# Four PSUM banks as one tile in rotation, and a gate spread in groups of eight tokens

## The chip, the cores and the metric

The kernel runs on one core of a Trainium2 chip. The metric is the device time of one execution in microseconds (us); smaller is better. The core has a matmul engine (TensorE, PE), which writes its results into PSUM, and VectorE (DVE), ScalarE (ACT) and GpSimd (POOL), which read them there. SyncE (SP) issues the transfers. PSUM has eight banks of 512 floats per partition. Each engine runs its own instructions in order and waits on semaphores for the others.

## The reference

A two-layer encoder over 256 tokens of width 1024. Layer 0 is differential attention and an expert mixer, layer 1 stick-breaking attention and an expert mixer. After each of the four parts comes a LayerNorm of `alpha * x + f(x)`. The expert mixer is the large part:

```python
q = (xt @ w_pq).reshape(T, PEER_HEADS, 2, PEER_HALF)
scores = jnp.einsum('thcd,hckd->thck', q, sub_keys).astype(jnp.float32)
s_top, i_top = lax.top_k(scores, PEER_TOPK)
cand = s_top[:, :, 0, :, None] + s_top[:, :, 1, None, :]
g_s, g_i = lax.top_k(cand.reshape(T, PEER_HEADS, PEER_TOPK * PEER_TOPK), PEER_TOPK)
expert_ids = jnp.take_along_axis(cand_ids.reshape(...), g_i, axis=-1)
gates = jax.nn.softmax(g_s, axis=-1)
...
h = jax.nn.gelu(jnp.einsum('td,ted->te', xblk, u_sel), approximate=False)
return jnp.einsum('te,ted->td', gb * h, v_sel)
```

Each token chooses 8 heads x 16 of 16384 experts (128 x 128 keys).

## The kernel before

The kernel computes the hidden values of all experts for all tokens, spreads the gates over a full 128 x 128 grid per token, and multiplies. A float32 product is done in three matmul passes: every weight tile is split into a high part `h` (ACT, L144) and a low part `l` (DVE or POOL, L149), and `h`, `l` and the low part of the input are multiplied in turn (L200 for products with 512 outputs, L245 for the query projection, L827, L840 and L842 for the hidden values). A matmul with `l` waits for the split.

PSUM is used through one pool with four buffers to a tag. Tag "w" serves the hidden values, the scores of the attention and the transposes of the LayerNorm; tag "acc" serves the accumulators of the projections and of the gather, the transposes of Q (L405), the V projection of layer 0 (L445, copied out by ACT in L449), two of the four head outputs of the attention (L505 and L507, read in L517 and L524), the routing scores (L674, copied by ACT in L675) and the gate spread. Each "acc" tile is one bank, and a new tile waits for the readers of the tile four before it. Most of the order of instructions is chosen by a scheduler; a few places are written out by hand.

Stages of a layer: attention, LayerNorm, query projection, then hidden values on PE with the routing on DVE beside them (scores, top 16 with MAX8, products, softmax), then the gate spread with more hidden values between, then the gather (L200 with weights `wh` and `wl`). A LayerNorm (L272 adds the accumulator, L275 and L294 are the statistics, L300 and L304 scale block 0 on ACT, L323 block 1 on DVE, L313 transposes) works on two blocks of 128 tokens. The matmuls before it are ordered so that block 0 is complete while the last matmuls of block 1 still run.

In the attention of layer 0, K is projected into "w" tiles while the rotary work on Q runs (L394 to L396 on DVE, L397 on POOL). Q is then transposed in four tiles, each of which is read by ACT (L407, the high part) and then DVE (L408, the low part). After K's projection comes V's (L445), and K's rotary work and transposes beside it.

The gate spread takes eight tokens at a time. DVE builds `oa` (L930: one where the key's second index matches), and `gh` and `gl` (L926: products of two small tables). PE multiplies them per token (L940, L941) into two accumulators of four tokens. The results of the last group are drained between `gh` and `gl` of the next: DVE multiplies the stored hidden values in (L899), ACT copies the rest (L900). The small tables (L913 to L916) are built for 16 tokens.

Of the kernel before, what the change touches and what calls it, by code (L numbers as in the profile page):

```python
# [20 lines left out]
P = 128  # L21
D = 1024
T = 256
# [35 lines left out]
def trunk(ctx: ExitStack, tc: tile.TileContext, x, xT, ln_g, ln_b, w_qkv, w_o_a, lam_p, subln, w_kv,  # L59
# [8 lines left out]

    big = bigp.tile([P, NE * T], F32, name="big")

    def reg(off, *shape):
# [16 lines left out]
    nc.vector.tensor_scalar(identb, jp, 0.0, None, OP.is_equal)  # L88
    ntri = const.tile([P, P], F32, name="ntri")
    nc.vector.tensor_scalar(ntri, jp, 0.0, -1.0, OP.is_le, OP.mult)  # L90
    none1 = const.tile([P, 1], F32, name="none1")
# [101 lines left out]
    def accs(tag):  # L193
        a = [[psum.tile([P, 512], F32, name=tag, tag=tag) for _ in range(NB)] for _ in range(2)]
        return [[a[f][b] for f in range(2)] for b in range(NB)]
# [38 lines left out]
    def stationary(xh, xl, src, tag, first=False):  # L234
        acc = [psum.tile([P, 2, T], F32, name=tag, tag=tag) for _ in range(4)]
        pre = units.prefetched() if first else []
        for d in range(DC):
            hl = pre[d] if d < len(pre) else units.get(src(d), "v" if first else "a", 1, units.after(d) if first else None)
            seq = [(n, q) for n in range(8) for q in range(2)] + [(n, 2) for n in range(8)]
            if first and d == 0:  # L240
                seq = [(n, q) for q in (0, 2, 1) for n in range(8)]
            for n, q in seq:
                w, a = hl[q // 2], (xh, xl, xh)[q]
                w, c = (w[n // 4], n % 4 * P) if isinstance(w, list) else (w, n * P)
                nc.tensor.matmul(acc[n // 2][:, n % 2, :], w[:, c:c + P], a[:, d, :],  # L245
                                 start=(d == 0 and q == 0 and n % 2 == 0),
                                 stop=(d == DC - 1 and q == 2), skip_group_check=True)
        return acc
# [127 lines left out]
    def diff_attention(xh, xl):  # L376
# [22 lines left out]
        def tr(srcv, dstT, tag):  # L399
            for i in range(4):  # L400
                pt = psum.tile([P, 2, T], F32, name=tag, tag=tag)
                for j in range(2):
# [96 lines left out]
        def s3(i):  # L499
            a = aT[i % 2]  # L500
            hs = slice(2 * i, 2 * i + 2)
            ps = psum.tile([P, 2, NB, P], F32, name="om", tag="acc" if i < 2 else "w")
            for j in range(2):
# [66 lines left out]

    def stick_breaking(xh, xl, yv, gb):
        QT, KT, V = reg(0, DC, T), reg(2048, DC, T), reg(4096, NB, D)
        spb = [reg(6144 + i * 512, 512) for i in range(4)]
# [75 lines left out]
    def peer(layer, xh, xl, spill, o_res):  # L649
# [16 lines left out]
        def scores(b):  # L666
            sc = reg(19456 + b * 2048, 2 * HP, NE)
            for g in range(4):
                ps = psum.tile([P, 4, NE], F32, name="acc", tag="acc")
                c = g % 2  # L670
                r = slice(c * 64, c * 64 + 64)
                for j in range(4):
                    h = 4 * (g // 2) + j
                    nc.tensor.matmul(ps[:, j, :], qp[r, h, b * P:(b + 1) * P], subk[r, h, :], start=True, stop=True)  # L674
                nc.scalar.activation(sc[:, 8 * (g // 2) + c:8 * (g // 2) + c + 7:2, :], ps, AF.Copy)  # L675
            return sc

        def routing(b, sc):
# [116 lines left out]
            yield 0.8  # L795
            pt = psum.tile([P, 4, P], F32, name="acc", tag="acc")
            for c in range(3):
# [85 lines left out]
        def extra():  # L883
            for i in range(N_STORED, N_STORED + N_EXTRA, 2):
                hx[i] = work.tile([P, 2 * T], F32, name="hx", tag="hw", bufs=RING)
                yield from hidden.pair(i, hx[i])

        ex = extra()
        nst = N_EXTRA * 24 - 48
# [5 lines left out]
        def drain():  # L895
            for t, ps in prev:
                pv = ps.rearrange("p t i -> p i t")
                wv = big.rearrange("p (i t) -> p i t", t=T)[:, :, t:t + 4]
                nc.vector.scalar_tensor_tensor(wv[:, 0:N_STORED], pv[:, 0:N_STORED], 1.0 / GS, wv[:, 0:N_STORED], OP.mult, OP.mult)  # L899
                nc.scalar.activation(wv[:, N_STORED:], pv[:, N_STORED:], AF.Copy, scale=1.0 / GS)  # L900

        i2 = iota2.unsqueeze(1).to_broadcast([P, 4, P, 2])
        NR = 8
        hi1, hi2, hi3 = (work.tile([P, NR, 8, 2], F16, name=n, bufs=1) for n in ("hi1", "hi2", "hi3"))
        lo = work.tile([P, NR, 16, 2], F16, name="lo", bufs=1)

        def parts(t0):
# [3 lines left out]

            i2 = iota2.unsqueeze(1).to_broadcast([P, NR, P, 2])
            nc.vector.tensor_tensor(hi1, i2[:, :, 0:8], col(1, 8), OP.is_equal)  # L913
            nc.vector.tensor_tensor(lo, i2[:, :, 0:16], col(2, 16), OP.is_equal)
            nc.vector.tensor_tensor(hi2, hi1, col(3, 8), OP.mult)
            nc.vector.tensor_tensor(hi3, hi1, col(4, 8), OP.mult)  # L916

        for t8 in range(0, T, 8):
# [15 lines left out]
            outer(oj, hi3)  # L934
            for r in range(2):
                ps = psum.tile([P, 4, NE], F32, name="acc", tag="acc")
                prev.append((t8 + 4 * r, ps))
                for k in range(4):
                    m, e = 2 * r + k // 2, k % 2
                    nc.tensor.matmul(ps[:, k, :], gh[:, m, :, e], oa[:, m, :, e], start=True, stop=False)  # L940
# [8 lines left out]

        acc = [[psum.tile([P, 512], F32, name="acc", tag="acc") for _ in range(2)] for _ in range(NB)]  # L950
        ext = list(range(N_STORED, N_STORED + N_EXTRA, 2))
# [157 lines left out]
```

## Time and profile before

| | |
|---|---|
| median of 3 runs | 1870.14 us (1869.6 to 1871.68) |
| the profiled execution | 1869.78 us, span 1868.0 us, so 1.78 us lie outside the span |
| TensorE (PE) busy | 1818.9 us, 97% of the span |
| VectorE (DVE) busy | 1311.6 us, 70% |
| ScalarE (ACT) busy | 920.4 us, 49% |
| GpSimd (POOL) busy | 176.6 us, 9% |
| mean granted clock of PE | 0.995 |

Layer 0 has its attention from 0 to about 130 us, the query projection from 134.5 to 157.6, routing to 280, the gate spread to about 404 and the gather to about 927. Layer 1 has its attention to about 1060, the projection from 1064 to 1088, routing to 1210, the gate spread to 1334 and the gather to 1858. The last LayerNorm ends the program. In the rows, `x4` after an instruction is a count, a number in brackets with an arrow is the time that the engine stood idle before it and who released it. Neighbouring instructions of an engine overlap in the records by a few hundredths to a tenth of a microsecond, so what an instruction costs its engine is read from start to start.

### The profile page before, as it was taken

The numbers are of one execution on the slowest core, as the hardware profiler recorded it, in microseconds if no ns is written. First come the engines' busy times: TensorE is split into PE (matmuls) and PEld (weight loads), VectorE is DVE, ScalarE is ACT, GpSimd is POOL, SyncE is SP. The second block draws the span as 40 slices with busy tenths as digits, with TensorE's granted clock in tenths as the row PEclk, the third lists the DMA queues.
The fourth block names the chain that finished last, engine by engine and source line by source line (L and its number), as shares of the span: only waits on it lengthen the run. The fifth ranks groups of instructions, "written<-read, shape, count | busy, mean of one in ns | idle before, by whom it ended". The sixth has DMA issues, their size and how long they took to land.

```text
span 1868.0 us, 29132 instructions
## 1 busy us (share of the span) xinstructions
PE 1818.9 (97%) x11304; PEld 1598.8 (86%) x11304; DVE 1311.6 (70%) x2522; ACT 920.4 (49%) x1244; POOL 176.6 (9%) x190
## 2 busy tenths in 40 slices
PE   8999999999999999999999999999999999999997
PEld 6889989998888888878798799899888888888886
DVE  5666989986666666665553569899866666666655
ACT  4645454554444444444447454545544444445442
POOL 5435200000000000000132251000000000000001
PEclk9999999999999999999999999999999999999999
DMA  6534644346666666676653356443566666666764
GB/s 217 175 136 146 183 147 147 114 144 195 189 201 186 181 192 192 189 259 192 203 158 103 125 157 185 146 146 108 153 193 191 182 185 191 194 194 185 259 192 134
DMA packets 90442, 325.28 MB, mean 174 GB/s; under 512 B 10176, under 2 KB 10560, under 8 KB 89664
## 3 DMA queue, kind: packets, MB, share of 16 engines
q1 hardware_dynamic: 90304, 323.43, 56.6%
q8 instruction: 88, 1.44, 0.3%
q14 instruction: 50, 0.41, 0.1%
HBM read 320.24 MB, written 3.15 MB: 173 GB/s over the span
## 4 chain that ended last, share of the span: by engine, by line
PE 80%; DVE 13%; issue 2%; DMA 2%; ACT 2%; POOL 1%; SPq 0%; ACTq 0%; POOLq 0%; DVEq 0%
PE acc L200 38%; PE w L827 12%; PE w L840 12%; PE w L842 6%; PE acc L245 4%; DVE l L149 4%; DVE gl L926 2%; DVE big L899 2%; DVE gh L926 2%; PE w L245 1%; DVE oa L930 1%; PE w L200 1%; PE acc L445 1%; DMA big<-in_ln_g 1%; ACT h L144 1%
## 5 line engine op out<-in xcount | busy, mean ns | idle before, releaser
L144 ACT ACTIVATE h<-raw 128x1024 fp32r<-128x1024 f32 x579 | 613.5, 1060 | 821.9 <-PE acc L200 333.7
L149 DVE TENSOR_TENSOR l<-raw,h 128x1024 fp32r<-128x1024 f32 x526 | 649.0, 1235 | 400.8 <-ACT h L144 396.6
L200 PE MATMUL acc<-l,wh 128*128 128x512 f32 x1024 | 400.5, 391 | 2.6 <-DVE l L149 2.6
L200 PE MATMUL acc<-h,wl 128*128 128x512 f32 x1024 | 400.4, 391 | 0.0
L827 PE MATMUL w<-xhl,h 128*128 128x256 f32 x2176 | 400.0, 286 | 0.3 <-ACT h L144 0.2
L840 PE MATMUL w<-xhl,h 128*128 128x512 f32 x960 | 340.0, 396 | 0.0
L827 PEld LDWEIGHTS w<-xhl,h 128*128 128x128 f32 x2176 | 338.1, 192 | 0.9 <-ACT h L144 0.7
L827 PE MATMUL w<-xhl,l 128*128 128x256 f32 x1088 | 308.3, 285 | 5.7 <-DVE l L149 5.5
L200 PE MATMUL acc<-h,wh 128*128 128x512 f32 x1024 | 279.0, 392 | 0.0
L842 PE MATMUL w<-xhl,l 128*128 128x256 f32 x960 | 268.8, 280 | 0.0
L200 PEld LDWEIGHTS acc<-l,wh 128*128 128x128 f32 x1024 | 192.3, 188 | 44.8 <-DVE l L149 3.4
L200 PEld LDWEIGHTS acc<-h,wl 128*128 128x128 f32 x1024 | 192.5, 188 | 37.6
L200 PEld LDWEIGHTS acc<-h,wh 128*128 128x128 f32 x1024 | 188.2, 188 | 39.9 <-ACT h L144 0.4
L840 PEld LDWEIGHTS w<-xhl,h 128*128 128x128 f32 x960 | 180.5, 188 | 42.5
L827 PEld LDWEIGHTS w<-xhl,l 128*128 128x128 f32 x1088 | 208.1, 192 | 7.6 <-DVE l L149 6.9
L842 PEld LDWEIGHTS w<-xhl,l 128*128 128x128 f32 x960 | 181.2, 189 | 6.2
L149 POOL TENSOR_TENSOR l<-raw,h 128x1024 fp32r<-128x1024 f32 x53 | 129.4, 2441 | 177.2 <-ACT h L144 167.8
L844 DVE TENSOR_REDUCE hx<-w 128x256 f32<-128x512 f32 x120 | 82.7, 690 | 38.9 <-PE w L842 38.7
L984 DVE TENSOR_TENSOR wl<-big,wh 128x512 fp32r<-128x512 f32 x128 | 86.9, 687 | 5.2 <-PE acc L200 4.7
L200 PE MATMUL acc<-h,xhl 128*128 128x512 f32 x256 | 84.2, 403 | 6.2 <-ACT h L132 4.8
L173 POOL TENSOR_TENSOR ahead<-big,ahead 128x512 fp32r<-128x512 f32 x12 | 16.5, 1402 | 744.0 <-ACT ahead L163 744.0
L983 ACT ACTIVATE wh<-big 128x512 fp32r<-128x512 f32 x128 | 77.7, 616 | 15.6 <-PE acc L200 11.1
(207 smaller groups left out, 1753.9 us busy)
## 6 DMA issues: line engine op xcount, KB each, us to landing
raw<-in_uT SPq DMA_DIRECT2D x256, 512.0 KB, 4.2
raw<-in_v SPq DMA_DIRECT2D x256, 512.0 KB, 4.2
raw<-in_w_qkv SPq DMA_DIRECT2D x23, 512.0 KB, 4.3
raw<-in_w_kv SPq DMA_DIRECT2D x12, 512.0 KB, 4.3
raw<-in_w_o_a SPq DMA_DIRECT2D x8, 512.0 KB, 4.2
big<-in_w_pq SPq DMA_DIRECT2D x8, 512.0 KB, 6.4
raw<-in_w_pq SPq DMA_DIRECT2D x8, 512.0 KB, 5.5
raw<-in_w_q SPq DMA_DIRECT2D x8, 512.0 KB, 4.1
```

The costliest lines, as they stand in the source:

```text
L144: self.h = nc.scalar.activation(h, raw, AF.Copy)
L149: o = e.tensor_tensor(l, raw, h.bitcast(F32), OP.subtract)
L200: nc.tensor.matmul(acc[b][f], a[:, d, ts], w[:, fs], start=(first and q == 0), stop=(last and q == 2))
L245: nc.tensor.matmul(acc[n // 2][:, n % 2, :], w[:, c:c + P], a[:, d, :], start=(d == 0 and q == 0 and n % 2 == 0), stop=(d == DC - 1 and q ...
L827: nc.tensor.matmul(ps[:, k, :], w[:, ds], a[:, d, :], start=(d == 0 and q == 0), stop=(d == DC - 1 and q == 2))
L840: nc.tensor.matmul(ps, h[:, ds], both[:, d].rearrange("p c t -> p (c t)"), start=(d == 0), stop=False, skip_group_check=True)
L842: nc.tensor.matmul(ps[:, 0:T], l[:, ds], xh[:, d, :], start=False, stop=(d == DC - 1), skip_group_check=True)
L844: nc.vector.tensor_reduce(dst[:, k * T:(k + 1) * T], ps.rearrange("p (c t) -> p t c", t=T), axis=AX.X, op=OP.add)
L899: nc.vector.scalar_tensor_tensor(wv[:, 0:N_STORED], pv[:, 0:N_STORED], 1.0 / GS, wv[:, 0:N_STORED], OP.mult, OP.mult)
L926: nc.vector.tensor_tensor(dst.rearrange("p r (a b) t -> p r a b t", b=16), hi[:, rs].unsqueeze(3).to_broadcast([P, 4, 8, 16, 2]), lo[:, rs ...
L983: nc.scalar.activation(wh, s, AF.Copy)
L984: nc.vector.tensor_tensor(wl, s, wh.bitcast(F32), OP.subtract)
```

## The change

Tag "acc" goes. One tile `quad` of four banks is allocated once, and a function hands out slices of it: one bank, or two neighbouring banks, in rotation. Tag "w" is as before. The gate spread uses two banks for eight tokens, with one drain on each engine of twice the elements. The small tables are built for 32 tokens, and one of the three high tables is overwritten in place. A constant triangle for layer 1 is built where it is used.

```diff
+    quad = psum.tile([P, 4, 512], F32, name="quad", bufs=1)
+    turn = [0]
+
+    def bank(tag, *shape):
+        n = int(np.prod(shape))
+        if tag == "w":
+            t = psum.tile([P, n], F32, name="w", tag="w")
+        else:
+            k = (n + 511) // 512
+            assert turn[0] % k == 0
+            i = turn[0] % 4
+            turn[0] += k
+            t = quad[:, i:i + k, :].rearrange("p a b -> p (a b)")[:, 0:n]
...
-        a = [[psum.tile([P, 512], F32, name=tag, tag=tag) for _ in range(NB)] for _ in range(2)]
+        a = [[bank(tag, 512) for _ in range(NB)] for _ in range(2)]
...
-                pt = psum.tile([P, 2, T], F32, name=tag, tag=tag)
+                pt = bank(tag, 2, T)
...
-            ps = psum.tile([P, 2, NB, P], F32, name="om", tag="acc" if i < 2 else "w")
+            ps = bank("acc" if i < 2 else "w", 2, NB, P)
...
-                ps = psum.tile([P, 4, NE], F32, name="acc", tag="acc")
+                ps = bank("acc", 4, NE)
...
-                wv = big.rearrange("p (i t) -> p i t", t=T)[:, :, t:t + 4]
+                wv = big.rearrange("p (i t) -> p i t", t=T)[:, :, t:t + 8]
...
-        NR = 8
-        hi1, hi2, hi3 = (work.tile([P, NR, 8, 2], F16, name=n, bufs=1) for n in ("hi1", "hi2", "hi3"))
+        NR = 16
+        hi2, hi3 = (work.tile([P, NR, 8, 2], F16, name=n, bufs=1) for n in ("hi2", "hi3"))
...
-            nc.vector.tensor_tensor(hi1, i2[:, :, 0:8], col(1, 8), OP.is_equal)
+            nc.vector.tensor_tensor(hi2, i2[:, :, 0:8], col(1, 8), OP.is_equal)
             nc.vector.tensor_tensor(lo, i2[:, :, 0:16], col(2, 16), OP.is_equal)
-            nc.vector.tensor_tensor(hi2, hi1, col(3, 8), OP.mult)
-            nc.vector.tensor_tensor(hi3, hi1, col(4, 8), OP.mult)
+            nc.vector.tensor_tensor(hi3, hi2, col(4, 8), OP.mult)
+            nc.vector.tensor_tensor(hi2, hi2, col(3, 8), OP.mult)
...
-            for r in range(2):
-                ps = psum.tile([P, 4, NE], F32, name="acc", tag="acc")
-                prev.append((t8 + 4 * r, ps))
-                for k in range(4):
-                    m, e = 2 * r + k // 2, k % 2
+            ps = bank("acc", 8, NE)
+            prev.append((t8, ps))
+            for k in range(8):
+                    m, e = k // 2, k % 2
```

The change moves instructions and waits in places that the diff does not touch. The rows below are of the built programs, and the lines of the changed one are 15 higher in the first two places (L272 is L287, L405 is L420, L445 is L460) and 19 higher in the third (L674 is L693, L827 is L846). The first place is DVE at the LayerNorm after the layer-0 attention, before:

```order
L272 SCALAR_TENSOR_TENSOR big<-big,acc 128x512 [waits PE_49] x2
L275 BN_STATS st<-big 128x6 [waits DVE_49] x2
L294 BN_AGGR mv<-st 128x2 [waits DVE_49]
L295 TENSOR_SCALAR mv<-mv 128x1 [waits DVE_49]
L272 SCALAR_TENSOR_TENSOR big<-big,acc 128x512 [waits PE_49]
L300 SCALAR_TENSOR_TENSOR nmr<-mv 128x1 [waits Pool_49]
L275 BN_STATS st<-big 128x6 [waits DVE_49]
L272 SCALAR_TENSOR_TENSOR big<-big,acc 128x512 [waits PE_49]
```

And the same place now:

```order
L287 SCALAR_TENSOR_TENSOR big<-big,quad 128x512 [waits PE_49]
L287 SCALAR_TENSOR_TENSOR big<-big,quad 128x512
L290 BN_STATS st<-big 128x6 [waits DVE_49] x2
L309 BN_AGGR mv<-st 128x2 [waits DVE_49]
L310 TENSOR_SCALAR mv<-mv 128x1 [waits DVE_49]
L287 SCALAR_TENSOR_TENSOR big<-big,quad 128x512
L315 SCALAR_TENSOR_TENSOR nmr<-mv 128x1 [waits Pool_49]
L290 BN_STATS st<-big 128x6 [waits DVE_49]
L287 SCALAR_TENSOR_TENSOR big<-big,quad 128x512
```

Before, every add waits for the matmuls of its own bank. Now only the first waits, and what it waits for is the last matmul of all four banks. The three other LayerNorms read alike.

The second place is PE in the layer-0 attention, where K's projection ends (L200 into "w") and V's begins (L445). Before:

```order
L200 MATMUL w<-l,xhl 128x512
L200 MATMUL w<-h,xhl 128x512
L445 MATMUL acc<-h,xhl 128x512 [waits Activation_49]
L445 MATMUL acc<-h,xhl 128x512 [waits PE_49]
L445 MATMUL acc<-l,xhl 128x512 [waits DVE_49]
```

And now (`quad<-ident,big` are transposes of Q, `w<-ident,big` of K):

```order
L215 MATMUL w<-h,xhl 128x512
L420 MATMUL quad<-ident,big 128x128 [waits DVE_49]
L420 MATMUL quad<-ident,big 128x128 x3
L420 MATMUL w<-ident,big 128x128 [waits PE_49,Pool_49]
L420 MATMUL w<-ident,big 128x128 [waits DVE_49,PE_49]
L420 MATMUL w<-ident,big 128x128 [waits DVE_49,PE_49,Pool_49]
L420 MATMUL w<-ident,big 128x128 [waits DVE_49,PE_49]
L420 MATMUL w<-ident,big 128x128 [waits Pool_49]
L420 MATMUL w<-ident,big 128x128 x5
L420 MATMUL quad<-ident,big 128x128 [waits DVE_49]
L420 MATMUL quad<-ident,big 128x128 x3
L460 MATMUL quad<-h,xhl 128x512 [waits DVE_49]
```

V's first matmul came right behind K's last. Now two groups of Q's transposes and all of K's stand between, and V's first matmul waits for the DVE subtraction of the last Q tile (L408 before).

The third place is PE at the routing scores of layer 0. Before:

```order
L827 MATMUL w<-xhl,l 128x256 [waits Pool_49]
L674 MATMUL acc<-big 128x128 [waits DMAHW0_49,Activation_49]
L674 MATMUL acc<-big 128x128
L674 MATMUL acc<-big 128x128 [waits Activation_49]
L674 MATMUL acc<-big 128x128
L674 MATMUL acc<-big 128x128 [waits PE_49]
```

And now, with the hidden-value matmuls between two groups of scores cut:

```order
L693 MATMUL quad<-big 128x128 [waits DMAHW0_49,Activation_49]
L693 MATMUL quad<-big 128x128 x3
L846 MATMUL w<-xhl,h 128x256
...
L846 MATMUL w<-xhl,l 128x256
L693 MATMUL quad<-big 128x128 [waits Activation_49]
L693 MATMUL quad<-big 128x128 x3
```

The score matmuls stood together. Now each group of four waits for ACT, and about 28 hidden-value matmuls stand between two groups.

## Rows read from the trace of the kernel before

**Rows 1.** The page: shares of the chain that ended last, by engine.
```profile
PE 80%; DVE 13%; issue 2%; DMA 2%; ACT 2%; POOL 1%; SPq 0%; ACTq 0%; POOLq 0%; DVEq 0%
```
**Rows 2.** Windows: length, busy PE, PEld, DVE, ACT, POOL, then PE clock, DMA, GB/s.
```profile
62.40:104.00 41.60, 40.40 (x251) 34.49 (x250) 28.51 (x62) 28.13 (x89) 14.33 (x55) 0.88 0.43 137
...
157.60:280.00 122.40, 118.44 (x992) 116.64 (x991) 108.87 (x491) 63.09 (x78) 28.85 (x12) 1.00 0.53 160
...
296.00:310.00 14.00, 13.18 (x141) 12.72 (x139) 14.00 (x34) 6.78 (x12) 0.00 (x0) 1.00 0.38 114
...
464.00:790.00 326.00, 326.00 (x1643) 275.29 (x1642) 214.69 (x234) 154.62 (x176) 0.00 (x0) 1.00 0.63 189
...
1064.00:1088.00 24.00, 24.00 (x193) 24.00 (x192) 14.10 (x23) 11.20 (x16) 6.74 (x50) 0.95 0.46 147
```
**Rows 3.** Waits of PE in the gate spread, 283 to 410: total, times, longest.
```profile
PE acc L941 <- DVE gl L926: 6.0, 9, 0.7
```
**Rows 4.** DVE in order of time, last LayerNorm: start, length, instruction, idle before.
```profile
1853.35 1.37 DVE L272 SCALAR_TENSOR_TENSOR big<-big,acc 128x512 f32<-128x512 f32 x2 [1.08 <-PE acc L200]
...
1857.07 0.69 DVE L275 BATCH_NORM_STATS2 st<-big 128x6 f32<-128x512 f32 x1
1858.11 0.69 DVE L272 SCALAR_TENSOR_TENSOR big<-big,acc 128x512 f32<-128x512 f32 x1 [0.35 <-PE acc L200]
...
1859.56 0.21 DVE L294 BATCH_NORM_AGGREGATE mv<-st 128x2 f32<-128x12 f32 x1
```
**Rows 5.** PE in order of time: the last matmul of the program.
```profile
1857.68 0.39 PE L200 MATMUL acc<-h,wl 128*128 128x512 f32 x1
```
**Rows 6.** PE in order of time, LayerNorm after the layer-1 attention.
```profile
1062.93 1.89 PE L313 MATMUL w<-ident,big 128*128 128x128 f32 x8 [1.33 <-DVE big L323]
```
**Rows 7.** DVE in order of time, gate spread of layer 0.
```profile
309.23 0.23 DVE L913 TENSOR_TENSOR hi<-iota,idxT 128x128 f16<-128x128 f16 x1
309.36 0.29 DVE L914 TENSOR_TENSOR lo<-iota,idxT 128x256 f16<-128x256 f16 x1
309.56 0.23 DVE L915 TENSOR_TENSOR hi<-hi,idxT 128x128 f16<-128x128 f16 x1
...
309.83 0.69 DVE L930 TENSOR_TENSOR oa<-iota,idxT 128x1024 f16<-128x1024 f16 x1
...
311.04 0.57 DVE L899 SCALAR_TENSOR_TENSOR big<-acc,big 128x168 f32<-128x168 f32 x2
311.52 0.69 DVE L926 TENSOR_TENSOR gl<-hi,lo 128x1024 f16<-128x1024 f16 x1
...
323.59 0.70 DVE L930 TENSOR_TENSOR oa<-iota,idxT 128x1024 f16<-128x1024 f16 x1
```
**Rows 8.** DVE in order of time, layer-0 attention, K's rotary work and after.
```profile
53.37 0.42 DVE L394 TENSOR_TENSOR big<-w,big 128x256 f32<-128x256 f32 x1 [1.71 <-PE w L200]
...
58.42 1.97 DVE L149 TENSOR_TENSOR l<-raw,h 128x1024 fp32r<-128x1024 f32 x1
...
63.65 1.28 DVE L408 TENSOR_TENSOR qk<-w,qk 128x512 fp32r<-128x512 f32 x2
```
**Rows 9.** PE in order of time: the first V matmuls.
```profile
54.53 0.62 PE L445 MATMUL acc<-h,xhl 128*128 128x512 f32 x2
```
**Rows 10.** Routing of layer 0 in order of time: PE, then DVE.
```profile
160.72 2.82 PE L674 MATMUL acc<-big 64*128 64x128 f32 x32
...
163.09 0.68 DVE L706 MAX8 big<-big 128x8 f32<-128x128 f32 x3 [0.26 <-ACT big L675]
...
253.46 0.28 DVE L792 TENSOR_REDUCE big<-big 128x8 f32<-128x128 f32 x1 [2.65 <-ACT big L791]
```
**Rows 11.** ACT in order of time, gate spread of layer 0.
```profile
310.01 1.06 ACT L144 ACTIVATE h<-raw 128x1024 fp32r<-128x1024 f32 x1 [1.83 <-issue]
...
311.45 0.80 ACT L900 ACTIVATE big<-acc 128x344 f32<-128x344 f32 x2
```
**Rows 12.** PE in order of time, one group of the gate spread, and after.
```profile
308.13 0.23 PE L940 MATMUL acc<-oa,gh 128*128 128x128 f16 x1
...
309.08 0.48 PE L827 MATMUL w<-xhl,h 128*128 128x256 f32 x2
```

More of the change, by code (lines that the diff above doesn't have):

```diff
@@ L69, in trunk @@
     big = bigp.tile([P, NE * T], F32, name="big")
+    quad = psum.tile([P, 4, 512], F32, name="quad", bufs=1)
[10 more added lines that the diff above has]
+            t = quad[:, i:i + k, :].rearrange("p a b -> p (a b)")[:, 0:n]
+        if len(shape) == 1:
+            return t
+        names = "abc"[:len(shape)]
+        return t.rearrange("p (%s) -> p %s" % (" ".join(names), " ".join(names)), **dict(zip(names[1:], shape[1:])))
     def reg(off, *shape):
@@ L88, in trunk @@
     nc.vector.tensor_scalar(identb, jp, 0.0, None, OP.is_equal)
-    ntri = const.tile([P, P], F32, name="ntri")
-    nc.vector.tensor_scalar(ntri, jp, 0.0, -1.0, OP.is_le, OP.mult)
     none1 = const.tile([P, 1], F32, name="none1")
@@ L234, in stationary @@
     def stationary(xh, xl, src, tag, first=False):
-        acc = [psum.tile([P, 2, T], F32, name=tag, tag=tag) for _ in range(4)]
+        acc = [bank(tag, 2, T) for _ in range(4)]
         pre = units.prefetched() if first else []
@@ L571, in stick_breaking @@
     def stick_breaking(xh, xl, yv, gb):
+        jn = reg(19456, P).bitcast(I32)
+        nc.gpsimd.iota(jn, pattern=[[1, P]], base=0, channel_multiplier=-1)
+        ntri = work.tile([P, P], F32, name="ntri", tag="oh", bufs=OH)
+        nc.vector.tensor_scalar(ntri, jn, 0.0, -1.0, OP.is_le, OP.mult)
         QT, KT, V = reg(0, DC, T), reg(2048, DC, T), reg(4096, NB, D)
@@ L795, in routing @@
             yield 0.8
-            pt = psum.tile([P, 4, P], F32, name="acc", tag="acc")
+            pt = bank("acc", 4, P)
             for c in range(3):
@@ L886, in extra @@
                 yield from hidden.pair(i, hx[i])
+        turn[0] += turn[0] % 2
         ex = extra()
@@ L947, in peer @@
         ctx2.close()
-        acc = [[psum.tile([P, 512], F32, name="acc", tag="acc") for _ in range(2)] for _ in range(NB)]
+        acc = [[bank("acc", 512) for _ in range(2)] for _ in range(NB)]
         ext = list(range(N_STORED, N_STORED + N_EXTRA, 2))
```

## The prediction

> **What bounds the kernel now.** Read first the chain that ended last [rows 1]: the reader is to see that it runs on TensorE (PE) for 80% and on VectorE (DVE) for 13%. A microsecond that PE stands still is therefore lost nearly everywhere. Then the busy time by stage [rows 2]. In the layer-0 attention PE works 40.40 of 41.60 us at a mean clock of 0.88, in the routing stretch 118.44 of 122.40, in the gather all 326.00 of 326.00. Only the gate spread is of another kind: DVE works 14.00 of 14.00 us and PE 13.18. There PE's waits [rows 3] are for `gl`, a DVE product, 6.0 us in 9 waits: DVE is the bound. So fewer DVE instructions pay in the gate, and waits put on PE cost elsewhere.
>
> **What the change is as built.** The diff speaks of the gate; the order speaks of the whole program. Four accumulators that were four tiles are now slices of one tile, and the order shows that a wait is now for the tile: in a LayerNorm only the first add waits for PE, and for the last matmul of both halves; the attention's first V matmul waits for DVE; each group of score matmuls waits for ScalarE (ACT). I price these places, then the gate.
>
> **LayerNorms (four).** Before, DVE does block 0's adds and statistics while PE runs block 1's last matmuls. In the final one [rows 4] the first add starts at 1853.35, block 1's first statistics at 1857.07, and the second add of block 1 at 1858.11, released by PE, whose last matmul ends at 1857.68 + 0.39 = 1858.07 [rows 5]. After it DVE needs 1859.56 − 1858.07 = 1.49 us to the aggregate. Now all of it stands behind that matmul. From the first add to the start of block 1's first statistics is 1857.07 − 1853.35 = 3.72, that instruction issues the next after about 0.65 (0.69 long, the overlap of two neighbours in these rows being a few hundredths), and from the second add to the aggregate is 1859.56 − 1858.11 = 1.45. Sum 5.82, where the same point came 1.49 − 0.04 = 1.45 behind: +4.37 there. The two of layer 0 lose a little less, since their last add waited longer already; **+4.25** each, 17 for four. PE has nothing else there, since the next matmuls need the normalised rows; in the final one the output follows, with no PE at all. Bounds: 16, if the two layer-0 ones hide a quarter us each more, and 18.5, if SBUF traffic of POOL slows DVE.
>
> These gaps are followed by PE at a lower clock in one place already: after the layer-1 attention the eight transposes took 1.89 us and the projection behind them ran at 0.95 [rows 2, 6], which is 5% of 24 us or 1.2 us. A gap four microseconds longer now stands at three such places: **+2**, between 0 (the clock as now) and 4 (each as costly as the one shown).
>
> **Layer-0 attention.** The Q transposes shared four tiles; now each of the four groups waits until ACT and DVE have read the group before. The last group waits for a DVE subtraction that DVE has queued behind K's rotary work, and the V matmuls, which wrote other banks at 54.53 [rows 9], wait for the subtraction after that. I follow DVE [rows 8]: the rotary work takes 58.42 − 53.37 = 5.05, with one subtraction (0.6) among it, then an `l` split of 1.23 to 1.97, a subtraction (half of 1.28), four transposes (about 0.55), an ACT copy of about the same, and the last subtraction: 5.05 + 0.6 + 1.6 + 0.64 + 0.55 + 0.6 + 0.64 = 9.7 us. K's matmuls end about 1.1 us earlier than before, since eight of the Q transposes now lie behind them. Of the 9.7 us PE fills about 1.1 with those eight and 2.2 with K's sixteen, and the rope starts 1.1 us ahead of the end of K's matmuls: PE stands for 9.7 − 1.1 − 3.3 = **5.3**. Of three later waits on the tile (V's last quarter behind the read of the first head output, head output 2 behind V's copies, the output projection behind the read of head output 2) I give the first nothing, since some forty matmul rows lie between, the others about 1 and 2; half a microsecond more goes to V matmuls that no longer fill holes of the scores. Sum **+9**. Below, 4: the stretch has PE at 0.88 of its clock, so part of the matmuls may only move into slower time that was there anyhow. Above, 15: the hole of 5.3 brings its own low clock, and all three waits open.
>
> **Routing scores.** Before, 32 score matmuls run in 2.82 us [rows 10] in one go. Now each group of four waits for the ACT copy of the last one, with some 28 hidden-layer matmuls between. The first group comes 13 such matmuls later (1.6 us), the second copy also stands behind an ACT GELU, so DVE's second MAX8 comes about 3.8 us after 163.09. DVE is nearly full there, so its end moves; two ACT waits of about 2.6 us near its end [rows 10] may swallow part. I take **+2** per layer, 4 in all; bounds 0 and 7.6.
>
> **Gate.** Four groups of eight tokens take 323.59 − 309.83 = 13.76 us of DVE, 3.44 each [rows 7]. Start to start, two drains take 311.52 − 311.04 = 0.48. One of twice the elements saves the fixed part of one: at 168 elements 0.24, of which about 0.17 grows with elements (512 outputs take 0.69, 168 take 0.33 long, so about 1 ns an element), leaving 0.065 saved. The tables take 0.60 for sixteen tokens (309.23 to 309.83); for 32 tokens three of 256 elements at 0.20 and one of 512 at about 0.34 make 0.94 instead of 1.20: 0.065 a group. Together 0.13 × 64 groups = **−8.4**. More than −12.8 it can't be: PE is busy 13.18 of 14.00, so its floor per group is 3.44 × 0.94 = 3.24. Against it stands the new wait: one bank group is in flight, and PE's next group waits for both drains of the last. DVE drain 0.4, the ACT drain behind it up to 0.8 [rows 11], PE's sixteen matmuls 309.08 − 308.13 = 0.95 [rows 12]: 2.2 us in a ring of 3.3, so only an ACT held by a 1.06 split and more makes it late. I give **+1**. Bounds of the gate together −12.8 and +8.
>
> The Trainium skill, Perfetto Trace Analysis, under Optimizing Scalar/DVE Operations, puts the fixed part of a DVE instruction on PSUM at about 125 ns. An estimate by that page makes the drains save 64 × 0.125 = 8 us instead of 4.2, and the sum would be 4 lower; I keep the starts of rows 7, which show the drains themselves.
>
> The gather keeps its matmuls in strict order, but `l` is ready microseconds ahead in a stretch where PE never waits: 0. V's copies in layer 1 end long before the next user: 0. The triangle built on POOL: 0.
>
> **Sum.** 17 + 2 + 9 + 4 − 8.4 + 1 = +24.6 on the execution's own 1869.78, which is 1894.4; the median of the runs lies 0.4 higher, so **1894**.
>
> **Rivals.**
> 1. *The waits stay with the bank.* Then the adds start as now and only the gate moves: 1869.78 − 7.4 = 1862, faster. It decides as soon as block 0's adds start before block 1's last matmul. The waits in the order speak against it: 3%. The Trainium skill, Perfetto Trace Analysis, under Matmuls, says that independent groups should rotate through banks so that the reading of one overlaps the matmuls of the next; the change rotates too, so by that rule alone this rival would be right and the time 1862; the waits in the order do not bear it out, and no run here shows it yet.
> 2. *The holes of the attention cost little*, because scores and exponentials there are a chain of latencies in which PE's lateness is made up: 9 becomes 2, 1887. For it the clock of 0.88, against it 40.40 of 41.60 busy: 17%.
> 3. *The gate goes into lockstep.* If ACT's 1.06 split or GELU stands before half of the drains, a ring becomes 2.2 + 1.06 + 0.57 = 3.8 against 3.3, half a microsecond in 32 groups: the gate gains nothing and loses 8, 1910. For it ACT's split 1.4 us ahead of a drain [rows 11]; against it ACT half idle: 13%.
> 4. *PE's clock falls for longer* after the longer gaps: 4 us at three places and as much in the attention, 1906: 10%.
>
> The forecast itself has 55%, and 2% go to what I don't see. The forecast's own range is 1885 to 1903; with the second rival whole and half of the third and fourth, 1878 to 1909 holds eight in ten. About 0.2% (3.7 us) can be told from no change: faster 4%, by rival 1 and a gate at its floor with the attention hidden; within 3%; slower 93%.
>
> **What would show it.** Right: a DVE add in each LayerNorm released by the last L200 matmul and an aggregate 5.8 us behind it; a PE hole of about 5 us before the first V matmul; score groups 3.5 us apart; gate periods of 3.3 us. Wrong: adds that start during block 1's matmuls; a gate whose PE waits name the ACT drain in most groups; an attention that ends no later than now.

## The result, and the profile after

The changed kernel takes 1928.19 us (median of 4 runs, 1925.24 to 1931.67) where the kernel before takes 1869.87 in the same comparison. The ratio is 1.031, 95% interval 1.0294 to 1.0325: slower by 58 us. The direction was forecast, the size was not: the range ended at 1909. The profiled execution took 1925.24 us with a span of 1923.5, 55.5 more than before. The page's first lines:

```profile
span 1923.5 us, 28973 instructions
...
PE 1841.4 (96%) x11304; PEld 1614.6 (84%) x11304; DVE 1311.6 (68%) x2394; ACT 916.3 (48%) x1180; POOL 175.5 (9%) x191
```

DVE issues 128 instructions fewer and is busy exactly as long as before. PE runs the same 11304 matmuls; it stands idle for 82.1 us instead of 49.1, and it is busy 22.5 us longer. The longer busy time goes with the clock: the mean granted clock is 0.984 here and 0.995 before, and 0.016 of 1923.5 us less 0.005 of 1868.0 us is about 21 us. So the loss has two parts, new waits and matmuls at the lower clock; up to 9 us of the second part lie in the first 130 us (clock 0.89, before 0.96). To find the waits, one compares the times at which the same instruction stands in both traces. The end of the last matmul ahead of each LayerNorm is such a mark, and the shift grows in steps:

| mark | before | after | shift |
|---|---|---|---|
| V's first matmul, layer 0 | 54.53 | 67.91 | +13.4 |
| last matmul of the layer-0 attention | 129.8 | 149.4 | +19.6 |
| first matmul of the query projection | 134.26 | 158.27 | +24.0 |
| second MAX8 of layer 0 | 163.09 | 193.01 | +29.9 |
| second group of the gate spread (`oa`) | 291.90 | 322.55 | +30.7 |
| last group of the gate spread (`oa`) | 395.85 | 427.78 | +31.9 |
| last matmul of the gather, layer 0 | 927.8 | 962.4 | +34.6 |
| last matmul of the layer-1 attention | 1059.9 | 1100.0 | +40.1 |
| last matmul of the program | 1858.1 | 1908.9 | +50.8 |
| end of the span | 1868.0 | 1923.5 | +55.5 |

The layer-0 attention lost 19.6 us where 9 were forecast. The waits of PE over the whole program show a line that did not exist before:

```profile
PE quad L959 <- ACT big L920: 19.6, 24, 1.5
PE w L328 <- ACT big L319: 15.3, 3, 5.1
...
PE w L509 <- ACT big L489: 3.6, 3, 2.9
```

(Lines of the changed kernel: L959 and L960 are the gate's matmuls, L920 is ACT's drain, L328 is the transpose of a LayerNorm.) The first row is the gate: in 24 of its 64 groups PE waits for the ACT drain of the group before, 19.6 us in all. [Rows 3] named `gl`, a DVE product, in this place.

**The LayerNorm** is as forecast. The last one, DVE in order of time, columns as in [rows 4]:

```profile
1908.88 1.28 DVE L287 SCALAR_TENSOR_TENSOR big<-big,quad 128x512 f32<-128x512 f32 x2 [5.84 <-PE quad L215]
...
1911.71 0.68 DVE L287 SCALAR_TENSOR_TENSOR big<-big,quad 128x512 f32<-128x512 f32 x1
...
1913.13 0.67 DVE L287 SCALAR_TENSOR_TENSOR big<-big,quad 128x512 f32<-128x512 f32 x1
...
1914.56 0.21 DVE L309 BATCH_NORM_AGGREGATE mv<-st 128x2 f32<-128x12 f32 x1
```

DVE stands 5.84 us, is released by the last matmul, and only then does all four adds. The aggregate comes 5.71 us after that matmul's end in each of the four, where it came 1.49 to 1.76 after it before.

**The hole ahead of V** in the layer-0 attention, five windows of 5 us (columns as in [rows 2]), then PE in order of time:

```profile
55.00:60.00 5.00, 3.67 (x19) 2.38 (x17) 3.97 (x10) 2.53 (x4) 4.32 (x3) 1.00 0.58 155
60.00:65.00 5.00, 3.10 (x12) 2.44 (x13) 3.53 (x6) 0.00 (x0) 4.05 (x3) 0.55 0.36 95
65.00:70.00 5.00, 3.59 (x13) 2.80 (x12) 2.83 (x5) 2.56 (x5) 0.00 (x0) 0.50 0.20 75
70.00:75.00 5.00, 5.00 (x14) 3.88 (x14) 0.25 (x1) 1.06 (x1) 0.32 (x1) 0.59 0.00 0
75.00:80.00 5.00, 5.00 (x30) 3.96 (x29) 1.23 (x1) 1.72 (x2) 2.07 (x1) 1.00 0.37 99
```

```profile
58.04 0.66 PE L420 MATMUL quad<-ident,big 128*128 128x128 f32 x4 [0.66 <-DVE qk L423]
59.05 0.64 PE L420 MATMUL w<-ident,big 128*128 128x128 f32 x2 [0.36 <-POOL big L412]
60.65 0.48 PE L420 MATMUL w<-ident,big 128*128 128x128 f32 x1 [0.96 <-POOL big L412]
61.91 1.73 PE L420 MATMUL w<-ident,big 128*128 128x128 f32 x7 [0.78 <-DVE big L411]
64.11 1.54 PE L420 MATMUL w<-ident,big 128*128 128x128 f32 x6 [0.47 <-POOL big L412]
65.44 1.06 PE L420 MATMUL quad<-ident,big 128*128 128x128 f32 x4
67.91 0.80 PE L460 MATMUL quad<-h,xhl 128*128 128x512 f32 x1 [1.41 <-DVE qk L423]
```

PE never stands long at one place; it is stopped six times for 4.6 us in all, and its clock is at half (0.50, which is 1.2 GHz) from about 61 to 74 us. Six transposes take 1.54 us there, where six of them took 0.82 before, and V's first 14 matmuls take 6.1 us from start to start instead of 3.2. In [rows 9] V's first matmul stood at 54.53.

**The scores.** DVE at the start of routing before, in order of time (the first of the two lines of MAX8; the second is in [rows 10]):

```profile
162.54 0.29 DVE L706 MAX8 big<-big 128x8 f32<-128x128 f32 x1 [12.24 <-ACT big L675]
```

And now DVE, then ACT, then PE:

```profile
188.62 0.30 DVE L725 MAX8 big<-big 128x8 f32<-128x128 f32 x1 [13.80 <-ACT big L694]
193.01 0.68 DVE L725 MAX8 big<-big 128x8 f32<-128x128 f32 x3 [4.10 <-ACT big L694]
```

```profile
192.38 0.60 ACT L694 ACTIVATE big<-quad 128x512 f32<-128x512 f32 x1 [0.34 <-PE quad L693]
```

```profile
186.79 1.16 PE L693 MATMUL quad<-big 64*128 64x128 f32 x8
...
191.19 1.16 PE L693 MATMUL quad<-big 64*128 64x128 f32 x8
```

MAX8 waits twice, 17.9 us where it was 12.5. The second wait is 4.10 long. It is for a copy on ACT, and ACT itself stood 0.34 us for PE's second group of scores. That group starts 4.40 us after the first, and PE has no wait between them: it runs the hidden-value matmuls that stand between two groups in its order. Before, the second MAX8 started 0.55 us after the first; here it is 4.39.

**The gate.** One of the late groups: ACT, then PE, then DVE, in order of time:

```profile
331.17 1.06 ACT L159 ACTIVATE h<-raw 128x1024 fp32r<-128x1024 f32 x1 [2.58 <-issue]
332.14 0.58 ACT L849 ACTIVATE hx<-w 128x512 f32<-128x512 f32 x1
332.62 0.74 ACT L920 ACTIVATE big<-quad 128x688 f32<-128x688 f32 x1
```

```profile
333.40 0.22 PE L959 MATMUL quad<-oa,gh 128*128 128x128 f16 x1 [1.48 <-ACT big L920]
```

```profile
334.59 0.51 DVE L919 SCALAR_TENSOR_TENSOR big<-quad,big 128x336 f32<-128x336 f32 x1 [0.75 <-PE quad L960]
```

The drain waits on ACT behind a weight split and a GELU, PE's next group waits 1.48 us for the drain, and DVE then waits 0.75 for PE. The period of the gate is 3.497 us in layer 0 and 3.503 in layer 1, against 3.441 and 3.442 before. It is the mean of the 24 groups from the fifth `oa` to the 29th, a stretch that holds whole rounds of table building in every kernel (one in two groups before, one in four now).

### The profile page after: what moved, and what is told of

It reads as the page before. It is cut to its first block, busy times and chain, and to the rows that moved or that the text cites. A ratio compares the mean times of both kernels' runs of the same rounds, so it can differ in the third digit from the quotient of the medians.

```text
span 1923.5 us, 28973 instructions
## 1 busy us (share of the span) xinstructions
PE 1841.4 (96%) x11304; PEld 1614.6 (84%) x11304; DVE 1311.6 (68%) x2394; ACT 916.3 (48%) x1180; POOL 175.5 (9%) x191
## 4 chain that ended last, share of the span: by engine, by line
issue 39%; PE 37%; DVE 1%; ACT 1%; DMA 0%; POOL 0%; SPq 0%; POOLq 0%; ACTq 0%
PE quad L215 20%; PE w L859 6%; PE w L861 3%; PE w L846 2%; PE quad L260 2%; PE w L260 1%; PE quad L693 0%; DMA big<-in_ln_g 0%; PE w L639 0%; PE w L610 0%; PE w L629 0%; DVE st L290 0%; ACT h L159 0%; DVE big L287 0%; PE w L328 0%
## 5 line engine op out<-in xcount | busy, mean ns | idle before, releaser
L846 PE MATMUL w<-xhl,h 128*128 128x256 f32 x2176 | 403.4, 286 | 2.0 <-ACT h L159 2.0
L215 PE MATMUL quad<-l,wh 128*128 128x512 f32 x1024 | 401.2, 392 | 2.6 <-DVE l L164 2.6
L215 PE MATMUL quad<-h,wh 128*128 128x512 f32 x1024 | 400.6, 391 | 0.0
L215 PE MATMUL quad<-h,wl 128*128 128x512 f32 x1024 | 399.5, 390 | 0.0
L846 PEld LDWEIGHTS w<-xhl,h 128*128 128x128 f32 x2176 | 338.6, 192 | 4.3 <-ACT h L159 2.8
L846 PE MATMUL w<-xhl,l 128*128 128x256 f32 x1088 | 307.4, 285 | 6.7 <-DVE l L164 6.7
L215 PEld LDWEIGHTS quad<-l,wh 128*128 128x128 f32 x1024 | 192.6, 188 | 44.2 <-DVE l L164 3.5
L215 PEld LDWEIGHTS quad<-h,wh 128*128 128x128 f32 x1024 | 192.5, 188 | 42.5
L215 PEld LDWEIGHTS quad<-h,wl 128*128 128x128 f32 x1024 | 192.7, 188 | 38.9
L846 PEld LDWEIGHTS w<-xhl,l 128*128 128x128 f32 x1088 | 207.8, 192 | 9.0 <-DVE l L164 8.4
L1003 DVE TENSOR_TENSOR wl<-big,wh 128x512 fp32r<-128x512 f32 x128 | 86.8, 686 | 10.9 <-ACT wh L1002 5.9
L215 PE MATMUL quad<-h,xhl 128*128 128x512 f32 x256 | 84.9, 407 | 6.1 <-ACT h L147 5.0
L959 PE MATMUL quad<-oa,gh 128*128 128x128 f16 x512 | 65.8, 219 | 19.6 <-ACT big L920 19.6
```

The lines of the kernel that those rows point to most:

```text
L215: nc.tensor.matmul(acc[b][f], a[:, d, ts], w[:, fs], start=(first and q == 0), stop=(last and q == 2))
L846: nc.tensor.matmul(ps[:, k, :], w[:, ds], a[:, d, :], start=(d == 0 and q == 0), stop=(d == DC - 1 and q == 2))
L1003: nc.vector.tensor_tensor(wl, s, wh.bitcast(F32), OP.subtract)
```

## The experiments

Each code cut shows the lines that matter here, and of the line MODE only the entries that change. All kernels but three (`tables`, `duo_block`, `duo_half`) hand out the four banks by stage: a function `use` closes the pool of accumulators and opens one of another form. "one" means four single tiles as before, "quad" the one tile of the change, "two" two tiles of two banks. Each is timed beside the kernel before.

**gate_pairs**: the change's gate alone, with two groups in flight.

```diff
+MODE = {"attention": "one", "wo": "one", "route": "one", "gate": "two", "gather": "one"}
...
-    quad = psum.tile([P, 4, 512], F32, name="quad", bufs=1)
+    banks = [None, None, None]
...
+        use(MODE["gate"])
...
```

> Single accumulator tiles in every stage as before; only in the gate spread two tiles of two banks each, one drain of 336 elements, tables for 32 tokens. Theory (what was lost is waits for a whole tile; fewer DVE instructions do pay): the gate period falls by the 0.13 us of the forecast times 64, so 1870 - 8 = 1862, and no PE wait for the ACT drain is left. Rival (the larger drains themselves cost, since ACT and PE wait for 688 elements in one piece): no gain or a loss, 1870 to 1875.

Measured: 1862.78 us against 1869.34, ratio 0.9961 (0.9947 to 0.9975). The period is 3.339 us in both layers, 0.102 below before. PE's waits in the gate shrink to one row:

```profile
PE duo L988 <- DVE gl L974: 0.3, 1, 0.3
```

So fewer DVE instructions do pay, once PE can start the next group while the last one is drained: 64 x 0.102 = 6.5 us, close to the 6.6 of the total. The forecast had 0.13 a group. Of its two halves the drains came as forecast: in the mean of layer 0's groups two took 0.482 us from start to start and one of twice the elements takes 0.418, 0.064 saved. The tables saved less. For 32 tokens they take 1.06 us where 0.94 was worked out (DVE, here from the changed kernel, in which these lines are the same):

```profile
331.49 0.28 DVE L933 TENSOR_TENSOR hi<-iota,idxT 128x256 f16<-128x256 f16 x1
331.69 0.41 DVE L934 TENSOR_TENSOR lo<-iota,idxT 128x512 f16<-128x512 f16 x1
332.02 0.28 DVE L935 TENSOR_TENSOR hi<-hi,idxT 128x256 f16<-128x256 f16 x1
332.34 0.29 DVE L936 TENSOR_TENSOR hi<-hi,idxT 128x256 f16<-128x256 f16 x1
332.55 0.68 DVE L950 TENSOR_TENSOR oa<-iota,idxT 128x1024 f16<-128x1024 f16 x1
```

The fourth of them overwrites the table that the third still reads, and it starts 0.32 us after the third, which is 0.28 long; the other two of this size are followed after 0.20 and 0.21. That the overwriting is the cause fits these rows and was not tested by itself. This version is 0.4% faster than the kernel before.

**gate_quad**: the same with one tile of four banks in the gate.

```diff
-"gate": "two"
+"gate": "quad"
```

> As gate_pairs, but in the gate spread the two halves in rotation belong to one tile of four banks. Theory (one group in flight, because the next group's first matmul waits for both drains of the last one): PE waits for the ACT drain about 20 us as in the changed kernel and the saving of DVE is lost, 1872 to 1878, some 12 us above gate_pairs. Rival (the loss in the changed kernel's gate came from what stands before it, the late scores): as gate_pairs, 1862.

Measured: 1875.33 us, ratio 1.0028 (1.0016 to 1.0041), 12.6 above gate_pairs. PE's and DVE's waits in the gate of layer 0:

```profile
PE quad L987 <- ACT big L948: 9.8, 12, 1.5
```

```profile
DVE big L947 <- PE quad L988: 4.9, 5, 1.6
```

Both are gone in gate_pairs, from which it differs only in the tile. What stands ahead of the gate is single tiles here, so late scores are not the cause: the theory holds.

**tables**: the kernel before with tables for 32 tokens alone; as in the change, one high table is overwritten in place and the triangle is built where it is used.

```diff
-        NR = 8
+        NR = 16
...
```

> The kernel before with only the small tables for 32 tokens (and the triangle of layer 1 built where it is used, for the space). Theory (start to start on a DVE that is full in the gate): 0.065 us a group, 4 us in all, 1866. Rival (PE, at 94% there, takes most of it): under 1 us, 1869 to 1870.

Measured: 1869.45 us, 1862.66 to 1872.51 in 10 runs, ratio 0.9994 (0.9979 to 1.0008): by the total, the rival. The gate says otherwise: its period is 3.403 us in both layers, 0.038 below before, 2.4 us in 64 groups where 4 were expected. In the profiled execution, the slowest of the ten, they were lost elsewhere: its layer-0 attention ends 2.6 us later than that of the kernel before. Two windows of the layer-0 attention, tables first, gate_pairs second:

```profile
90.00:100.00 10.00, 10.00 (x48) 8.54 (x48) 5.50 (x17) 4.95 (x21) 1.13 (x4) 0.50 0.00 0
```

```profile
90.00:100.00 10.00, 9.14 (x64) 8.11 (x64) 7.82 (x25) 7.08 (x29) 3.46 (x49) 0.83 0.01 2
```

In this stretch of scores and exponentials, which the edit doesn't touch, PE's clock is 0.50 in one trace and 0.83 in the other, and 48 or 64 matmuls get done. The two fastest runs of tables are the two with the highest mean clock. By itself this run shows the period and not the total.

**pairs_nr8**: gate_pairs with tables for 16 tokens.

```diff
-        NR = 16
+        NR = 8
...
```

> As gate_pairs, but with the small tables for 16 tokens as before. Theory (DVE alone sets the period of the gate): a period 0.065 us above gate_pairs', so 1863 + 4 = 1867, with the drain's half of the gain left. Rival (tables hide or do not count, as the total time of the run with tables alone could be read): 1863.

Measured: 1867.58 us, ratio 0.998 (0.9968 to 0.9991), 4.8 above gate_pairs, and a period of 3.376 and 3.377 us: 0.038 above gate_pairs, as much as the tables had given alone, where 0.065 was expected. By the periods the tables carry 0.038 of the 0.102 and the drains the rest. The total's 4.8 is more than 64 x 0.038 = 2.4; the kernel before took 1870.74 us beside this run and 1869.34 beside gate_pairs, and against it the difference is 3.4. The rest is not separated from the scatter.

**attn_quad**, then **attn_no_ln**: the one tile in both attentions with the LayerNorms behind them, then without these.

```diff
-MODE = {"attention": "one", "wo": "one", ...
+MODE = {"attention": "quad", "wo": "quad", ...      (attn_quad)
+MODE = {"attention": "quad", "wo": "one", ...       (attn_no_ln)
...
+        use(MODE["wo"])                             (attn_no_ln, ahead of both output projections)
```

> As gate_pairs, but the four banks of the accumulators are one tile in both attentions and the LayerNorms behind them (not in routing, gate or gather). Theory (waits for the whole tile in the layer-0 attention, and in two LayerNorms): 19.6 + 2 x 4.5 = 29 us above gate_pairs, 1890. Rival (the attention was late for another reason, such as the order of transfers): at most 9 us above it, 1871.

> As attn_quad, but the accumulators of the two output projections, which the LayerNorms read, are single tiles again. Theory (each LayerNorm pays 4.3 us for adds that wait for the last matmul of both blocks, and some clock behind it): 9 to 13 us below attn_quad's 1895, so 1882 to 1886, with the last add of block 0 during block 1's matmuls. Rival (the LayerNorm's delay hides behind the projection's weights): 1890 to 1895.

Measured: 1894.76 us, ratio 1.0129 (1.0107 to 1.015), and 1883.69, ratio 1.006 (1.0036 to 1.0083). The attentions alone cost 1883.69 − 1862.78 = 20.9 us, and it is the layer-0 attention that costs them: against gate_pairs the trace of attn_no_ln is 20.5 us late at its last matmul and 20.9 at that of the layer-1 attention. The two LayerNorms behind them cost 11.1 by the medians. Both theories hold. In the trace of attn_quad the projections behind the two LayerNorms start 4.4 and 4.3 us later after the last matmul than in gate_pairs, 8.7 together. The rest is not theirs by the traces: the layer-0 attention of attn_quad ends 2.6 us later than that of attn_no_ln, ahead of the LayerNorm.

**attn_tr_one** and **attn_v_one**: attn_no_ln with the Q transposes, or with V and the head outputs, on single tiles.

```diff
             if d == 5:
+                use("one")
                 tr(Q, QT, "acc")
+                use("quad")
```

```diff
+        use("one")
         av = accs("acc")
```

> As attn_no_ln, but the four Q transposes of layer 0 go to single tiles again; Q's projection, V's and the first two head outputs stay in one tile. Theory (the largest part of the attention's loss is the hole ahead of V's matmuls, since the fourth transpose group waits for DVE reads behind K's rotary work): V starts within 3 us of its old time instead of 13.6 late, and the total falls by 8 to 12 us from attn_no_ln's 1884, to 1872 to 1876. Rival (the loss comes from the later waits of V's last quarter and of the head outputs): 1880 to 1884.

> As attn_no_ln, but V's accumulators and the first two head outputs of layer 0 go to single tiles; Q's projection and its transposes stay in the one tile. Theory (the hole ahead of V comes from the transposes and stays, with its lower clock; the later waits go): 6 to 10 us below attn_no_ln's 1884, 1874 to 1878, with V's first matmul still over 10 us late. Rival (once PE is late at V, the rest follows whatever the tiles): 1881 to 1884.

Measured: 1873.63 us, ratio 1.0018 (1.0007 to 1.0029), and 1875.65, ratio 1.003 (1.0017 to 1.0042). V's first matmul in the one and in the other, PE in order of time:

```profile
56.24 0.39 PE L487 MATMUL quad<-h,xhl 128*128 128x512 f32 x1
```

```profile
67.88 0.79 PE L485 MATMUL acc<-h,xhl 128*128 128x512 f32 x1 [1.41 <-DVE qk L448]
```

The hole is the transposes' (10.1 us of 20.9); the later waits take 8.0; 2.8 are left. Q's projection in strict order is the candidate for them, but no run has it alone. Both theories hold, and neither rival.

**route_quad**, then **route_scores_one**: the one tile in projection and routing, then in the projection alone.

```diff
-"route": "one"
+"route": "quad"
...
             sc = reg(19456 + b * 2048, 2 * HP, NE)
+            use("one")                                (route_scores_one)
```

> As gate_pairs, but the four banks are one tile in the query projection and the routing. Theory (score groups of four wait for the copy of the group before, and DVE, nearly full there, ends that much later): 5 us a layer by the traces, so 1863 + 10 = 1873. Rival (the delay of the scores is swallowed by the slack between routing and the second group of the gate spread): 1863 to 1866.

> As route_quad, but the score groups (and the index transposes after them) go to single tiles again; only the query projection keeps the one tile. Theory (the score groups carry the whole loss of the routing stretch, because DVE is the chain there and each microsecond of its late start stays): back to gate_pairs, 1862 to 1864, and the wait of MAX8 for the score copies back from 17.9 to about 12.5 us. Rival (the projection's copies cost, too): 1868 to 1875.

Measured: 1874.82 us, ratio 1.0018 (1.0008 to 1.0028), 12.0 above gate_pairs; and 1868.92, ratio 0.9995 (0.9985 to 1.0005). DVE's wait for score copies in layer 0, in the first and the second:

```profile
DVE big L752 <- ACT big L721: 17.9, 2, 13.8
```

```profile
DVE big L753 <- ACT big L722: 14.1, 2, 13.9
```

In route_quad the second group of the gate comes 5.8 us (layer 0) and 6.7 (layer 1) later after the projection's start than in gate_pairs: the 5.4 of MAX8's waits stay whole. In route_scores_one the wait is 1.6 above gate_pairs' 12.5, since the first group of scores still waits for the projection's copies, and the gate comes 0.9 and 2.3 later. My expectation of a full return was wrong: it forgot that wait, and the rest of the 6 us (the clock in its layer-0 attention was 0.69 from 80 to 100 us, against 0.83 in gate_pairs) is not separated from the scatter.

**ln_quad**: the one tile in the two gathers.

```diff
-"gather": "one"
+"gather": "quad"
```

> As gate_pairs, but the four banks are one tile in the two gathers, which the two second LayerNorms read. Theory: 4.4 us for each LayerNorm, nothing in the gather, whose matmuls have their operands early, so 1863 + 9 = 1872, and up to 2 more for the clock behind the first of them. Rival (strict order in the gather costs, too): over 1876.

Measured: 1871.79 us, ratio 1.0002 (0.9989 to 1.0014), 9.0 above gate_pairs: two LayerNorms of 3.96 and 4.22 us by their aggregates, and nothing in the gather.

**duo_block** and **duo_half**: the changed kernel with two tiles of two banks in place of one of four; in the first a tile holds one block of tokens, in the second one half of the columns of both. For that the order in which the four accumulators take their banks changes, in the first for the projections, in the second for the gather.

```diff
-    quad = psum.tile([P, 4, 512], F32, name="quad", bufs=1)
+    duo = [psum.tile([P, 2, 512], F32, name="duo%d" % i, bufs=1) for i in range(2)]
-            t = quad[:, i:i + k, :].rearrange("p a b -> p (a b)")[:, 0:n]
+            t = duo[i // 2][:, i % 2:i % 2 + k, :].rearrange("p a b -> p (a b)")[:, 0:n]
...
-        a = [[bank(tag, 512) for _ in range(NB)] for _ in range(2)]               (duo_block)
-        return [[a[f][b] for f in range(2)] for b in range(NB)]
+        return [[bank(tag, 512) for _ in range(2)] for _ in range(NB)]
...
-        acc = [[bank("acc", 512) for _ in range(2)] for _ in range(NB)]           (duo_half)
+        acc = accs("acc")
```

> The changed kernel with two tiles of two banks instead of one of four, and the accumulators of a block of 128 tokens in one of them. Nothing else differs. Theory (waits go by tile): LayerNorms as before (20 us with their clock), two groups in flight in the gate (12 us), part of the score waits (5 us) and of the attention gone, so 1928 - 37 to 45 = 1883 to 1891. Rival (waits go by bank, and something else was slow): 1928.

> As duo_block, but each of the two tiles holds one half of the columns of both blocks of tokens, so that the first add needs the last matmul of the second block again. Theory (by tile): 16 to 22 us above duo_block from the four LayerNorms alone. By the other theory, that waits go by bank: the same as duo_block.

Measured: 1888.29 us, ratio 1.0084 (1.0061 to 1.0108), and 1897.99, ratio 1.014 (1.0113 to 1.0166). The four banks, the matmuls and the rotation are the same in all three kernels, and each accumulator has a bank of its own in all of them; what differs is which accumulators share a tile, and the order of instructions that follows from it. So waits go by tile, not by bank. The size of the second was missed: 9.7 us between them where 16 to 22 were expected. The last LayerNorm of duo_block, then of duo_half, DVE in order of time:

```profile
1873.63 1.28 DVE L286 SCALAR_TENSOR_TENSOR big<-big,duo 128x512 f32<-128x512 f32 x2 [1.76 <-PE duo L214]
...
1877.71 0.69 DVE L286 SCALAR_TENSOR_TENSOR big<-big,duo 128x512 f32<-128x512 f32 x1 [1.17 <-PE duo L214]
...
1880.48 0.21 DVE L308 BATCH_NORM_AGGREGATE mv<-st 128x2 f32<-128x12 f32 x1
```

```profile
1878.95 0.69 DVE L287 SCALAR_TENSOR_TENSOR big<-big,duo 128x512 f32<-128x512 f32 x1 [3.80 <-PE duo L215]
1880.99 0.69 DVE L287 SCALAR_TENSOR_TENSOR big<-big,duo 128x512 f32<-128x512 f32 x1 [1.35 <-PE duo L215]
...
1886.06 0.21 DVE L309 BATCH_NORM_AGGREGATE mv<-st 128x2 f32<-128x12 f32 x1
```

In duo_block the third add waits for the last matmul too (1.17), since both halves of block 1 share a tile, and the aggregate comes 2.80 us after that matmul; in duo_half the first add starts 2 us ahead of it, and the aggregate comes 5.12 after. The difference is 2.3 a LayerNorm, 9.3 in four, close to the 9.7 of the totals. The expectation for duo_block had its LayerNorms as before, which they are not: their aggregates come 2.80 us after the last matmul where it was 1.49 to 1.76.

## Why the prediction missed

The parts, each measured above gate_pairs or between two runs, add up: 1862.8 + 12.6 (gate tile) + 20.9 (layer-0 attention) + 11.1 + 9.0 (LayerNorms) + 12.0 (routing) = 1928.4, against 1928.2 measured. That they agree so closely is luck. The kernel before, timed beside each run, had medians from 1869.0 to 1870.7, and with each run set against its own, the parts come to 56.2 us above the kernel before where 58.3 were measured. Set beside the forecast:

| step | forecast | measured |
|---|---|---|
| LayerNorms and the clock behind them | +17 and +2 | +20.1 by the runs, 16.4 by the four aggregates |
| layer-0 attention | +9 | +20.9 |
| routing scores | +4 | +12.0 |
| gate: fewer DVE instructions | −8.4 | −6.6 |
| gate: one group in flight | +1 | +12.6 |

- **Waits go by tile**: right, and it carries the whole result. Rival 1, waits by bank, is out.
- **LayerNorms**: right in place and size, 5.71 us where 5.8 was worked out. The clock behind them did less: the first transposes ran at half speed (1.97 us for eight), but the window of the layer-1 projection, at 0.95 in [rows 2], is at 0.99 now, and the projections start 4.1 to 4.4 us later after the last matmul, which leaves at most half a microsecond for it. The projection of layer 0 then runs at 0.98 for 24 us, another half.
- **Fewer DVE instructions**: the drains came as forecast, 0.064 a group; the term of the tables was sized too high, 0.038 a group where 0.065 was worked out. Together 6.6 us instead of 8.4.
- **The gate** is the step that failed by most: "2.2 us in a ring of 3.3, so only an ACT held by a 1.06 split and more makes it late. I give +1". The ring was right and so was what makes it late; how often was not looked up. In [rows 11] the split ends 0.4 us ahead of a drain, and the row left out between them is a GELU:

```profile
310.98 0.57 ACT L830 ACTIVATE hx<-w 128x512 f32<-128x512 f32 x1
```

  A drain right behind a split, with or without a GELU between, comes back in three of eight groups: 12 of 32 groups of a layer are late, up to 1.5 us. PE has little slack to make it up (13.18 of 14.00 in [rows 2]). This was the third rival, given 13%; its gate was 8 us above before, and 6 were measured.
- **The attention** failed as a size: "PE stands for 5.3", "Sum +9". K's last matmul came 2.7 us late where the forecast had it 1.1 early (Q's projection, whose order is strict now, has done 13 matmuls instead of 16 when an `l` that it used to step around comes at 12.5 us, and from 12 to 20 us the clock is 0.79 where it was 1.00). From there to V's first matmul it is 10.9 us, where 9.7 − 1.1 = 8.6 had been worked out. PE stands for 4.6 us of it, near the forecast's 5.3; the transposes between, most of them at half the clock, take the rest. The clock at half from 61 to 74 us was named only as an upper bound, and it costs V's first 14 matmuls 3 us more. Then 59 V matmuls instead of 36 stand between the first scores and the output projection, and PE waits 5.0 us there in five places (1.2 in the kernel before) where I gave 3.5.
- **The scores** failed by a halving: "two ACT waits near its end may swallow part. I take +2 per layer". Nothing was swallowed: the second group of the gate comes 5.8 and 6.7 us later in route_quad. The two delays of 1.6 and 3.8 are also two waits and not one, so the whole price is 5.4 a layer; the upper bound was 7.6 in all. The groups came 4.4 us apart where 3.5 had been named.
- The bounds were too narrow as well: 20.9 lies above the attention's 15 and 12.0 above the scores' 7.6; only the gate's +6 against before (1875.33 − 1869.34) lies in its own, −12.8 to +8. In each of the three a wait was taken as partly hidden, on an engine that was busy for 89 to 97% of its stretch in [rows 2].
- The second rival, given 17%, is out: it had 2 us for the attention. Of the fourth, given 10%, the part in the attention came true, the part behind the LayerNorms did not.

## What to carry to other kernels

One tile over several banks makes one object for every wait: a read of one bank waits for writes to the others, and a write waits for all reads. Batch the drain over two banks if the reader is the bound, but keep two such tiles, so that one is filled while the other is drained (here 12.6 us between the two). Before a layout change is priced, look at every user of the tiles, and charge a new wait in full wherever the engine that waits is busy for nearly all of its stretch, as the three were here.

## What was not expected of the hardware

The granted clock of PE in the stretch of scores and exponentials of the layer-0 attention differs between traces of programs that do the same work there: from 90 to 100 us it is 0.67 in the kernel before, 0.50 with tables and 0.83 with gate_pairs. The ten runs of tables lie between 1862.66 and 1872.51 us, with mean clocks from 0.991 to 0.999. How much of that scatter comes from this stretch, no run here shows, since only one execution of each kernel was traced. A gain of 4 us is read in the stretch where it is made, and not from a few totals. And the stretch should hold whole rounds of whatever comes back only every few groups: counted over 30 groups, with 15 table builds before and 7 of twice the size now, the gain of `tables` looks like 0.06 to 0.07 us a group instead of 0.038.

In the hole ahead of V, where PE ran a few transposes at a time with waits between, the clock fell to half, and it was back at 1.00 in the window from 75 us, when V's matmuls had run without a wait since 67.91.
